# Strassen FFN weight sums moved from VectorE to accumulating DMA, with more FFN tiles in Strassen form

## The chip, the cores and the metric

One core of a Trainium2 chip runs the whole program. The metric is the device time of one execution in microseconds (us). TensorE (PE) multiplies, VectorE (DVE) and ScalarE (ACT) do elementwise work, GpSimd (POOL) does a little of it, and SyncE (SP) issues nearly all DMAs.

## The reference, cut to what matters

Two layers act on 512 latent tokens (x) and 256 context tokens (ctx), 1024 channels wide. Each has a mixer (four kinds of attention-like heads) and then a SwiGLU feed-forward network (FFN), which is what the change touches. In layer 1 only x goes through the FFN.

```python
def swiglu(h, w_ffn_in, w_ffn_out):          # 1024 -> 2 x 2816 -> 1024
    gate, up = jnp.split(h @ w_ffn_in, 2, axis=-1)
    return (jax.nn.silu(gate) * up) @ w_ffn_out

x = x + g2 * swiglu(modulate(rmsnorm(x, norm2), sh2, sc2), w_ffn_in, w_ffn_out)
if need_ctx:                                 # layer 0 only
    ctx = ctx + cg2 * swiglu(modulate(rmsnorm(ctx, norm2), csh2, csc2), w_ffn_in, w_ffn_out)
```

## The kernel before

Every float32 operand of a matrix product is scaled, split into a high and a low float16 part, and multiplied in three passes (high x high, high x low, low x high). Tokens stand in three groups of 256: group 0 is ctx, groups 1 and 2 are x.

**FFN weight tiles.** Each layer has 22 input tiles ("I", 128 hidden units: 1024 rows by 128 gate and 128 up columns) and 12 output tiles ("F", four column blocks by three chunks c of the hidden width). A tile is loaded by SP as two halves of 512 KB (`load_w`, `dma_thread2`); the F tiles of c = 2 have three row blocks instead of four, so their halves are 384 KB. At most four such halves of fast tiles are live at once (quota "wf", `wf1` = 4).

**Two ways to multiply a tile.** A *plain* tile is split by `split_thread` into float16 parts and multiplied by `p_ffn_in` (line 2168) or `p_ffn_out`: an input tile takes 48 matmuls of 128x256 for each group of tokens. A *fast* tile uses one level of Strassen-Winograd over its four quadrants A11, A12, A21, A22 and over token halves (x: group 1 against group 2; ctx: its own halves). `split_fast` builds seven operands: the quadrants A11, A12, A22 and the sums S1 = A21+A22, S2 = S1-A11, S3 = A11-A21, S4 = A12-S2. Each sum is one float32 `tensor_tensor` (`tto`, line 430; VectorE or GpSimd). Each operand is then split by `put`: a scaled cast to float16 (`cpo`, line 418 on ACT, or DVE) and one `scalar_tensor_tensor` for the low part (`sto`, line 434, DVE). `p_ffn_pair` (line 2208) and `p_out_pair` (line 2272) multiply: seven products of 12 matmuls, 84 in all, 256 columns wide for x and 128 for ctx, where a plain tile takes 96 for x. `pair_ev` (lines 2026 to 2039) and `resid_pair` (from line 995) join the products; `ffn_ev` (lines 2015 and 2016) ends a plain input tile. `pair_sums` and `hid_pair` make the sums on the token side.

**Which tiles are plain.** The tuple `cl` lists plain input tiles: three in layer 0, twelve in layer 1, so 15. Of the output tiles one is plain (layer 1, column block 3, c = 2).

**Order of the work.** `Plan.run` is a list scheduler that runs when the program is built. It holds a cost and a due time for each operation, picks an engine for operations that have several (`either`), and writes out a fixed order for each engine; each engine then runs its own order and waits at semaphores. Weight splits run ahead of the products: at most 16 tiles of split operands (quota "wh"; a fast tile takes four) exist at once. Where the scheduler foresees a gap of more than 0.4 us on PE, it fills it with dummy matmuls (`warm`, line 2466). So time on line 2466 is idle time of PE that looks busy.

Of the kernel before, what the change touches and what calls it, by code (L numbers as in the profile page):

```python
# [14 lines left out]
NL = 2  # L15
# [10 lines left out]
TUNE = {'pb': 2, 'pbr': 1, 's': 2, 'sr': 1, 't': 2, 'tr': 1, 'o': 3, 'orr': 1, 'bs': 6, 'bq': 4, 'p32': 3, 'sch': 4, 'lv': 3, 'pr_ap': 5, 'pr_av': 2, 'pr_cp': 7, 'pr_gate': 7, 'pr_bq': 10, 'pr_bv': 6, 'pr_du': 12, 'pr_ds': 6, 'pr_aatt': 6, 'pr_asc': 6, 'pr_catt': 10, 'pr_csc': 6, 'pr_gates': 2, 'pr_blev': 5, 'pr_bjoin': 4, 'pr_bst': 8, 'pr_bfin': 6, 'pr_norm': 0, 'pr_resid': 6, 'pr_split': 13, 'pr_prod': 20, 'win_prod': 16, 'pr_ffn': 1, 'pr_mod0': 3, 'pr_mod1': 1, 'win': 6, 'wmix': 8, 'wffn': 8, 'wkeep': 6, 'off1': 0, 'off2': 1, 'off0': 1, 'b_dve': 0.0, 'b_pool': 0.3, 'b_act': -0.2, 'm_pe': 0.0, 'm_el': 0.0, 'm1': 14, 'g2r': 2, 'pf': 8, 'wx': 2, 'wf1': 4, 'pr_ps': 2, 'x3': 2, 'jg': (1, 0), 'f32': ('B', 'B'), 'cl': ((0, 1, 19), (0, 1, 2, 3, 4, 6, 8, 10, 12, 14, 16, 18)), 'ofirst': 1, 'ostag': 0, 'clead': 0, 'ldma': 1.8, 'fgap': 0.4, 'fend': 0.1, 'hres': 3, 'bwh': 0.6, 'bws': 0.0, 'bpc': 0.0, 'bhh': 0.6, 'bhl': 0.0, 'pc': 3, 'flag': 1, 'pfr': 0, 'fst': 0, 'ord': 1, 'm0': 0, 'wsp': ((1, 1, 1, 1, 2, 1, 1, 1), (1, 1, 2, 1, 1, 1, 0, 2)), 'bwp': 0.3, 'bwl': 0.6, 'mcp': 1, 'm16': 0, 'm1n': 1, 'bmo': 1.5, 'bfu': 0.8, 'pr_rc': -1, 'ino': (2, 0), 'flag2': 4, 'mem': (28, 28), 'bfo': 0.0, 'pr_fin': 21, 'nlate': (1, 0, 1, 1, 1), 'bmc': 0.5}  # L26
# [25 lines left out]
W_OUT0 = 11  # L52

# [44 lines left out]
class Plan:  # L98
# [117 lines left out]
    def run(self):  # L216
        done, eng = self.done, self.eng
        while True:
# [56 lines left out]
            fin = end + (TUNE["ldma"] if e == "dma" else 0.0)  # L275
# [4 lines left out]
            for k in o.writes:  # L280
                done[k] = (fin, e)
# [55 lines left out]
def kernel(ctx: ExitStack, tc: tile.TileContext, xg, wall, wmod, pk32, pk16, dftx, dftc, out):  # L337
# [30 lines left out]
    modG = [const.tile([128, 2, 2, 8], F32, name=f"modG{l}") for l in range(NL)]  # L368
    lamt = const.tile([128, NL], F32, name="lamt")
# [76 lines left out]
    def load_w(l, i):  # L446
        n = w_rows(i)
        srcs = [wall[l, i, :, 0:n, :], wall[l, i, :, 4:4 + n, :]]
        add_load(("w", l, i), 2, None, None, srcs, ("wf", TUNE["wf1"] if fast(l, i) else 2))

    def dma_thread2():
        for key, n, shape, dt, srcs, quota, after in loads:
            ts = []
            if after:
                yield wait(*after)
            if key == "pk32b":
                yield op("dma", c_dma(4 * (NP32 - EARLY)), [], [key], lambda: nc.sync.dma_start(p32[:, EARLY:NP32], pk32[:, EARLY:NP32]))
                continue
            for i in range(n):
                if key[0] == "w":  # L460
                    t = yield alloc("g", [128, w_rows(key[2]), 256], F32, 0, quota)
# [28 lines left out]
    def split_fast(l, i):  # L490
# [3 lines left out]
        R = []  # L494
        A = {}
# [3 lines left out]
        def pair(a):  # L499
            for ab in PACK:  # L500
                if ab[0] == a:
                    t = yield alloc("g", [128, 2, 2, 4, 128], F16, w_reserve, ("wh", 16))
                    for u, name in enumerate(ab):
                        A[name] = t[:, u]
                        st["WT", l, i, name] = t
                    uses[id(t)] = users * len(ab)

        def put(name, src, key):
            yield from pair(name)
# [5 lines left out]
        st["A", l, i] = A  # L515
        yield wait(ld[0])
        R.append(st["ld", ("w", l, i), 0])
        a11, a21 = R[0][:, :, 0:128], R[0][:, :, 128:256]
        k = ("SS", l, i)
        yield from put("A11", a11, ld[0])  # L520
        yield wait(ld[1])
        R.append(st["ld", ("w", l, i), 1])
        a12, a22 = R[1][:, :, 0:128], R[1][:, :, 128:256]
        t = yield alloc("ff", [128, nr, 128], F32)
# [4 lines left out]
        t3 = yield alloc("ff", [128, nr, 128], F32)  # L529
        yield tto(n, [ld[0]], [k + (3,)], lambda: dict(out=t3, in0=a11, in1=a21, op=ALU.subtract), TUNE["bws"])  # L530
        yield from put("S3", t3, k + (3,))
        plan.free(t3)
        plan.free(R[0])
        yield from put("A12", a12, ld[1])
        yield tto(n, [("SA", l, i, "S2")], [k + (4,)], lambda: dict(out=t, in0=a12, in1=t, op=ALU.subtract), TUNE["bws"])
        yield from put("S4", t, k + (4,))
        plan.free(t)
        yield from put("A22", a22, ld[1])
        plan.free(R[1])

    WSP = {(l, i): TUNE["wsp"][l][min(i // 2, 7)] for l in range(NL) for i in range(NW)}

    def split_thread():
        for l in range(NL):
            for i in range(NW):
# [36 lines left out]
    def mod_chunk(l, c):  # L582
# [310 lines left out]
    def pair_sums(l, pr):  # L893
# [13 lines left out]
        for q in range(2):  # L907
# [5 lines left out]
            def make(n, o, x, y, rd):  # L913
                yield tto(2 * w, rd, [k + (n,)], lambda: dict(out=o, in0=x, in1=y, op=ALU.subtract))
# [4 lines left out]
            yield from make(1, a1, a2, a1, [hk[1, q], hk[2, q]])  # L919
            yield from make(3, a2, b2, a2, [hk[2, q + 2], k + (1,)])  # L920
            yield from make(2, a1, b2, a1, [("ST", l, pr, 1, q), hk[2, q + 2]])
# [51 lines left out]
    def add_to(x, p, j, l, g, src):  # L973
        kk = 2 * p + j
        return dict(out=x[:, j], in0=src, scalar=modG[l][:, 1, 1 if g == 0 else 0, kk:kk + 1], in1=x[:, j], op0=ALU.mult, op1=ALU.add)
# [12 lines left out]
    def resid_pair(l, p, c, pr):  # L988
# [10 lines left out]
        yield vop(c_dve(2 * w), [k + ("c",), k + ("P7",)], [k + ("u",)], lambda: V.tensor_tensor(out=t, in0=t, in1=Y, op=ALU.add))  # L999
# [14 lines left out]
        def f2():  # L1014
            V.scalar_tensor_tensor(**add_to(x2, p, 1, l, g2, v))
# [3 lines left out]
        def f3():  # L1019
            V.tensor_tensor(out=s[:, 0], in0=u, in1=Y[:, 1], op=ALU.add)  # L1020
            V.scalar_tensor_tensor(**add_to(x1, p, 1, l, g1, s[:, 0]))
# [930 lines left out]
    def hid_pair(l, j, pr):  # L1952
# [43 lines left out]
        yield tto(w, [k + (11,)] + ka, [k + ("t1",)], lambda: dict(out=a1, in0=a2, in1=a1, op=ALU.subtract))  # L1996
# [3 lines left out]
        yield from split(2 * w, (tc_[:, :, 0], tc_[:, :, 1]), a, [k + ("t2",)], k + (3,))  # L2000
# [19 lines left out]
    def pair_ev(l, m, X, Y, pr):  # L2020
# [5 lines left out]
        yield vop(c_dve(2 * w), [k + ("c",), k + ("P7",)], [k + ("u",)], lambda: V.tensor_tensor(out=c, in0=c, in1=Y, op=ALU.add))  # L2026
# [128 lines left out]
    def p_ffn_in(l, m, g):  # L2155
# [62 lines left out]
    def p_ffn_out(l, p, g, c):  # L2218
# [6 lines left out]
        for cb in range(2):  # L2225
            for j in js:
# [373 lines left out]
```

## Time and profile before

| | |
|---|---|
| median of 3 runs | 1724.01 us (1721.34 to 1727.58) |
| the profiled execution | 1723.17 us, span 1721.1 us |
| PE, DVE, ACT, POOL busy | 96%, 86%, 57%, 9% of the span |
| granted TensorE clock | 0.995 |
| moved by DMA | 201.43 MB |

An engine's busy time leaves out its waits. The FFN of layer 0 lies at about 490 to 1010 us of the span and that of layer 1 at about 1368 to 1700 us. The mixers lie before them.

### The profile page before, as it was taken

The page shows a single profiled execution, that of the slowest core. Times are in us where ns is not written, and L with a number is a line of the kernel's source. Part 1 is how long each engine was busy: PE and PEld are TensorE (multiplying, and loading weights), DVE is VectorE, ACT ScalarE, POOL GpSimd, SP SyncE. Part 2 cuts the span into 40 slices and gives each one's busy share as a digit, 9 for nine tenths or more (in the row PEclk, how much of TensorE's full clock was granted, in tenths as well). Part 3 has the DMA queues.
Part 4 walks back from the last instruction along what each step waited for, and adds up shares of the span by engine and source line. Part 5 has one row for each costly group of instructions (what it writes and reads, how often), then busy time and mean ns, then how long its engine had stood idle before and what let it go on. Part 6 is the DMA issues. An engine that isn't in the chain of part 4 may idle for free.

```text
span 1721.1 us, 45963 instructions
## 1 busy us (share of the span) xinstructions
PE 1660.1 (96%) x19718; PEld 1442.3 (84%) x19718; DVE 1484.4 (86%) x3141; ACT 979.6 (57%) x1766; POOL 149.7 (9%) x179
## 2 busy tenths in 40 slices
PE   8999998999999999999999999899889999999998
PEld 6678887887988788899889988788778888888887
DVE  6879899998589887899889998999997788888897
ACT  5637885566364553355435483678955555465454
POOL 0212111230000000000000013430010000000000
PEclk9999999999999999999999999999999999999999
DMA  9822111245135644522362351001113333462531
GB/s 368 334 83 79 59 46 52 86 149 185 50 124 187 193 148 122 174 75 63 111 193 72 112 179 36 14 27 50 51 51 123 136 95 102 127 193 75 184 124 50
DMA packets 62860, 201.43 MB, mean 117 GB/s; under 512 B 6848, under 2 KB 9152, under 8 KB 62656
## 3 DMA queue, kind: packets, MB, share of 16 engines
q1 hardware_dynamic: 62656, 198.50, 35.0%
q8 instruction: 154, 2.52, 0.6%
q14 instruction: 50, 0.41, 0.1%
HBM read 178.55 MB, written 19.92 MB: 115 GB/s over the span
## 4 chain that ended last, share of the span: by engine, by line
PE 59%; DVE 27%; ACT 6%; DMA 4%; issue 3%; POOL 1%; SPq 0%; DVEq 0%; ACTq 0%; POOLq 0%
PE ps L2208 15%; PE ps L2049 10%; DVE g L430 7%; PE ps L2168 7%; PE ps L2054 6%; PE ps L2272 5%; DVE g L434 4%; PE ps L616 2%; DMA g<-xsc 2%; PE ps L2466 2%; PE ps L1218 2%; DVE pl L430 1%; ACT g L418 1%; PE ps L1158 1%; DVE g L1548 1%
## 5 line engine op out<-in xcount | busy, mean ns | idle before, releaser
L430 DVE TENSOR_TENSOR g<-g,g 128x512 f32<-128x512 f32 (+7 forms) x698 | 439.9, 656 | 46.8 <-ACT g L416 34.4
L418 ACT ACTIVATE g<-g 128x512 f16<-128x512 f32 (+2 forms) x391 | 241.5, 642 | 236.3 <-DVE g L430 230.6
L2208 PE MATMUL ps<-g,g 128*128 128x256 f16 (+1 forms) x4032 | 361.4, 251 | 0.0
L2208 PEld LDWEIGHTS <-g 128*128 128x128 f16 x4032 | 326.2, 98 | 38.3 <-issue 10.9
L434 DVE SCALAR_TENSOR_TENSOR g<-g,g 128x512 f16<-128x512 f32 (+4 forms) x442 | 300.4, 696 | 59.0 <-ACT g L418 56.0
L2049 PE MATMUL ps<-g,g 128*128 128x256 f16 x2256 | 271.8, 273 | 1.8 <-DVE g L434 1.5
L2272 PEld LDWEIGHTS <-g 128*128 128x128 f16 x2709 | 226.0, 98 | 32.9 <-issue 8.2
L2049 PEld LDWEIGHTS <-g 128*128 128x128 f16 x2256 | 217.9, 98 | 29.2 <-DVE g L434 2.1
L2272 PE MATMUL ps<-g,g 128*128 128x256 f16 (+1 forms) x1917 | 211.0, 269 | 8.3 <-DVE g L999 3.6
L416 ACT CAST g<-g 128x512 f16<-128x512 f32 (+3 forms) x269 | 162.5, 615 | 76.3 <-DVE g L430 46.4
L2054 PE MATMUL ps<-g,g 128*128 128x256 f16 x1632 | 198.2, 274 | 0.0
L2054 PEld LDWEIGHTS <-g 128*128 128x128 f16 x1632 | 157.2, 98 | 31.3 <-issue 10.7
L2168 PE MATMUL ps<-g,g 128*128 128x256 f16 x1584 | 175.7, 273 | 0.0
L2168 PEld LDWEIGHTS <-g 128*128 128x128 f16 x1584 | 154.8, 98 | 18.9 <-issue 0.8
L416 ACT COPY g<-ps 128x512 f32<-128x512 f32 (+4 forms) x163 | 94.0, 583 | 120.2 <-PE ps L2272 23.7
L1198 ACT ACTIVATE g<-ps 128x512 f32<-128x512 f32 x156 | 91.6, 596 | 31.8 <-PE ps L1232 23.1
L430 DVE TENSOR_TENSOR pl<-g,ph 128x512 f16<-128x512 f32 x137 | 93.0, 694 | 7.1 <-ACT ph L416 6.7
L430 DVE TENSOR_TENSOR g<-g 128x256 f32<-128x256 f32 (+3 forms) x197 | 88.9, 460 | 2.4 <-ACT g L754 1.8
L430 POOL TENSOR_TENSOR g<-g,g 128x256 f16<-128x256 f32 (+4 forms) x17 | 23.5, 1385 | 695.0 <-ACT g L416 579.1
L416 ACT CAST ph<-g 128x512 f16<-128x512 f32 (+2 forms) x141 | 80.3, 572 | 4.7 <-DVE g L430 1.0
L2466 PE MATMUL ps<-p16c 128*128 128x256 f16 x595 | 75.5, 279 | 3.8 <-DMA p16c<-in_pk_dram 3.8
L2466 PEld LDWEIGHTS <-p16c 128*128 128x128 f16 x595 | 58.9, 101 | 15.8 <-issue 4.2
(248 smaller groups left out, 2220.2 us busy)
## 6 DMA issues: line engine op xcount, KB each, us to landing
g<-in_wall_dram SPq DMA_DIRECT2D x180, 512.0 KB, 4.4
g<-in_wmod_dram SPq DMA_DIRECT2D x96, 512.0 KB, 6.7
g<-xsc SPq DMA_DIRECT2D x40, 256.0 KB, 5.2
xsc<-g SPq DMA_DIRECT2D x40, 256.0 KB, 3.0
g<-in_xg_dram SPq DMA_DIRECT2D x12, 512.0 KB, 6.7
g<-in_wall_dram SPq DMA_DIRECT2D x16, 384.0 KB, 3.4
xsc<-g SPq DMA_DIRECT2D x10, 512.0 KB, 2.8
g<-xsc SPq DMA_DIRECT2D x10, 512.0 KB, 5.1
```

The source lines that it names most:

```text
L416: S.copy(o, i)
L418: S.activation(out=o, in_=i, func=AF.Copy, scale=scale)
L430: return either(r, w, ("dve", c_dve(n), lambda: V.tensor_tensor(**f()), bias, True), ("pool", c_pool(n), lambda: G.tensor_tensor(**f()), 0 ...
L434: return vop(c_dve(n), r, w, lambda: V.scalar_tensor_tensor(**f()), True)
L616: T.matmul(bank[32 * cg:32 * cg + 32, :], lhsT=cst[:, 2 * (4 * kr + cg):2 * (4 * kr + cg) + 32], rhs=ts[cg // 2][:, cg % 2, :], start=(kr ...
L1198: yield aop(c_act(512), [k], [k + (0,)], lambda pp=pp, bank=bank: S.activation(out=pp, in_=bank, func=AF.Exp, scale=scale), "exp")
L2049: T.matmul(bank[:, cb, :], lhsT=W[a][:, kw, 128 * cb:128 * cb + 128], rhs=xh[b][:, kx, :], start=(first and n == 0), stop=(last and n == 2 ...
L2054: T.matmul(bank[:, t, :], lhsT=xh[b][:, k, 128 * t:128 * t + 128], rhs=wt[a][:, k, :], start=(first and n == 0), stop=(last and n == 2), s ...
L2168: T.matmul(bank[:, cb, :], lhsT=wt[a][:, k % 4, :], rhs=xh[b][:, k % 4, :], start=(k == 0 and n == 0), stop=(k == 7 and n == 2), skip_grou ...
L2208: T.matmul(into[name], lhsT=wt[:, y, kk, :], rhs=x[:, z, kk, :], start=(name in ("P1", "P6") and kk == 0 and n == 0), stop=(kk == 3 and n ...
L2272: T.matmul(o, lhsT=wt[:, y, j % 4, :], rhs=x[:, z], start=(name in ("P1", "P6") and j == js[0] and n == 0), stop=(j == js[-1] and n == 2), ...
L2466: T.matmul(t[:, 0:256], lhsT=ident16, rhs=p16[:, 128:384], start=True, stop=True)
```

## The change

The two halves of a fast tile are laid out by quadrant in DRAM (a new input `wffn`), so that a quadrant is one contiguous run of each partition. Three of the four sums no longer have tiles of their own: GpSimd issues DMAs that read a quadrant from DRAM again and add it to what lies in SBUF. On the upper half R[0], A11 is split first, then A21 is added to it in place (S3); in the other place of R[0], which holds A21, A22 is added (S1), then A11 (S2), then A12 (S4), each after the operand before it has been split. An accumulating DMA only adds, so the signs of some operands turn; the token sums and the joining operations turn with them (`subtract` for `add`, a negated gate vector `modN`, scalar `-IWS`). In `hid_pair` one subtraction over two blocks becomes two operations of half the width. The scheduler books such a DMA as 1.5 us of GpSimd's time (`acp`) and 3.0 us until it has landed (`acl`). The list `cl` of plain input tiles becomes two in layer 0 and four in layer 1, so 6 instead of 15.

```diff
-'jg': (1, 0), 'f32': ('B', 'B'), 'cl': ((0, 1, 19), (0, 1, 2, 3, 4, 6, 8, 10, 12, 14, 16, 18))
+'acp': 1.5, 'acl': 3.0, 'whq': 16, 'pr_sp': 12, 'jg': (1, 0), 'f32': ('B', 'B'), 'cl': ((0, 1), (0, 1, 2, 3))
...
+        def quad(h, q):
+            return wffn[l, i - W_FFN0, :, h, q, 0:nr, :]
...
+        def acc(dst, src, rd, key):
+            yield ("op", (("pool", TUNE["acp"], lambda: G.dma_start(dst, src, accum_op=ALU.add), 0.0, False, None, TUNE["acl"]),), rd, [key])
...
+        def first():
+            a = R[0][:, 0]
+            k = ("SS", l, i, 3)
+            yield from put("A11", a, ld[0])
+            yield from acc(a, quad(0, 1), [("SA", l, i, "A11")], k)
+            yield from put("S3", a, k)
+            over(0)
+
+        def chain():
+            t = R[0][:, 1]
+            k = ("SS", l, i)
+            yield from acc(t, quad(1, 1), [ld[0]], k + (1,))
+            yield from put("S1", t, k + (1,))
+            yield from acc(t, quad(0, 0), [("SA", l, i, "S1")], k + (2,))
+            yield from put("S2", t, k + (2,))
+            yield from acc(t, quad(1, 0), [("SA", l, i, "S2")], k + (4,))
+            yield from put("S4", t, k + (4,))
+            over(0)
...
-        yield tto(n, ld, [k + (1,)], lambda: dict(out=t, in0=a21, in1=a22, op=ALU.add), TUNE["bws"])
-        yield from put("S1", t, k + (1,))
-        yield tto(n, [("SA", l, i, "S1")], [k + (2,)], lambda: dict(out=t, in0=t, in1=a11, op=ALU.subtract), TUNE["bws"])
-        yield from put("S2", t, k + (2,))
...
-        yield tto(n, [ld[0]], [k + (3,)], lambda: dict(out=t3, in0=a11, in1=a21, op=ALU.subtract), TUNE["bws"])
-        yield from put("S3", t3, k + (3,))
...
-        yield tto(n, [("SA", l, i, "S2")], [k + (4,)], lambda: dict(out=t, in0=a12, in1=t, op=ALU.subtract), TUNE["bws"])
-        yield from put("S4", t, k + (4,))
...
-        yield tto(2 * w, [k + (1,)] + kb + ([k + (12,)] if tail else []), [k + ("t2",)], lambda: dict(out=a, in0=b2.unsqueeze(1).to_broadcast([128, 2, w]), in1=a, op=ALU.subtract))
+        yield tto(w, [k + ("t1",)] + kb + ([k + (12,)] if tail else []), [k + ("t3",)], lambda: dict(out=a2, in0=a2, in1=b2, op=ALU.subtract))
+        yield tto(w, [k + (1,)] + kb, [k + ("t2",)], lambda: dict(out=a1, in0=a1, in1=b2, op=ALU.add))
```

## Rows read from the trace of the kernel before

**Rows 1.** Page, busy time, share of span and instructions of each engine
```profile
span 1721.1 us, 45963 instructions
PE 1660.1 (96%) x19718; PEld 1442.3 (84%) x19718; DVE 1484.4 (86%) x3141; ACT 979.6 (57%) x1766; POOL 149.7 (9%) x179
```

**Rows 2.** Busy time of each engine in both FFN stretches (layer 0, layer 1)
```profile
core 0: us, PE busy (x) PEld busy (x) DVE busy (x) ACT busy (x) POOL busy (x), PEclk, DMA share, GB/s
490.00:1010.00 520.00, 512.41 (x5888) 454.98 (x5887) 457.88 (x1023) 258.13 (x555) 3.55 (x4) 1.00 0.43 135
1368.00:1690.00 322.00, 318.97 (x2908) 284.06 (x2907) 279.49 (x520) 165.54 (x308) 0.70 (x1) 1.00 0.39 123
```

**Rows 3.** The same stretches, the dummy matmuls of line 2466 alone
```profile
490.00:1010.00 520.00, 21.84 (x179) 17.30 (x179) 1.00 0.43 135
1368.00:1690.00 322.00, 15.49 (x127) 12.42 (x127) 1.00 0.39 123
```

**Rows 4.** Groups of matmuls by line and form: count, busy us, mean ns
```profile
L2208 PE MATMUL ps<-g,g 128*128 128x256 f16 x2436 | 274.9, 273 | 0.0
L2168 PE MATMUL ps<-g,g 128*128 128x256 f16 x1584 | 175.7, 273 | 0.0
L2208 PE MATMUL ps<-g,g 128*128 128x128 f16 x1596 | 92.9, 219 | 0.0
```

**Rows 5.** Groups on DVE by line and form
```profile
L430 DVE TENSOR_TENSOR g<-g,g 128x512 f32<-128x512 f32 x321 | 216.7, 684 | 13.8 <-ACT g L754 3.8 <-ACT g L416 3.7 <-ACT g L1582 2.7
L434 DVE SCALAR_TENSOR_TENSOR g<-g,g 128x512 f16<-128x512 f32 x315 | 211.8, 686 | 51.8 <-ACT g L418 50.9
L430 DVE TENSOR_TENSOR g<-g,g 128x1024 f16<-128x1024 f32 x53 | 64.5, 1219 | 8.5 <-ACT g L416 7.9
L430 DVE TENSOR_TENSOR g<-g 128x256 f32<-128x256 f32 x99 | 41.1, 418 | 2.3 <-ACT g L754 1.8
L434 DVE SCALAR_TENSOR_TENSOR g<-g,g 128x512 f32<-128x512 f32 x29 | 19.9, 688 | 1.7
L2026 DVE TENSOR_TENSOR g<-g,ps 128x512 f32<-128x512 f32 x29 | 19.7, 680 | 3.0 <-PE ps L2208 3.0
L2016 DVE SCALAR_TENSOR_TENSOR g<-ps,g 128x256 f32<-128x256 f32 x33 | 13.8, 417 | 1.9 <-ACT g L2015 1.7
L2036 DVE TENSOR_TENSOR g<-g,ps 128x256 f32<-128x256 f32 x29 | 12.0, 415 | 2.0 <-PE ps L2208 2.0
L430 DVE TENSOR_TENSOR g<-g,g 128x384 f32<-128x384 f32 x21 | 11.5, 550 | 0.1
L430 DVE TENSOR_TENSOR g<-g 128x128 f32<-128x128 f32 x42 | 11.3, 283 | 0.1
L423 DVE CAST g<-g 128x512 f16<-128x512 f32 x36 | 15.0, 423 | 2.7 <-ACT g L416 1.5 <-ACT g L864 0.7
```

**Rows 6.** Groups on ACT by line and form
```profile
L418 ACT ACTIVATE g<-g 128x512 f16<-128x512 f32 x314 | 188.3, 625 | 209.9 <-DVE g L430 204.2 <-DVE g L434 4.1 <-issue 1.1
L561 ACT ACTIVATE g<-g 128x1024 f32<-128x1024 f32 x60 | 63.0, 1051 | 6.6 <-DMA g<-in_wall_dram 6.6
L416 ACT CAST g<-g 128x1024 f16<-128x1024 f32 x50 | 52.2, 1044 | 1.0
L416 ACT COPY g<-ps 128x512 f32<-128x512 f32 x101 | 57.9, 582 | 46.7 <-PE ps L616 13.5 <-PE ps L1808 13.3 <-PE ps L2272 6.6
```

**Rows 7.** Waits of ACT, layer 0 stretch, then layer 1: us, times, longest
```profile
ACT g L418 <- DVE g L430: 125.1, 86, 4.7
...
ACT g L418 <- DVE g L430: 104.1, 72, 3.9
```

**Rows 8.** The DMA queue of SP, then issues: count, KB, median us to landing
```profile
q1 hardware_dynamic: 62656, 198.50, 35.0%
...
g<-in_wall_dram SPq DMA_DIRECT2D x180, 512.0 KB, 4.4
g<-in_wmod_dram SPq DMA_DIRECT2D x96, 512.0 KB, 6.7
g<-xsc SPq DMA_DIRECT2D x40, 256.0 KB, 5.2
...
g<-in_dftc_dram SPq DMA_DIRECT2D x1, 256.0 KB, 2.4
```

**Rows 9.** Waits of DVE for residual loads, and of PE: us, times, longest
```profile
DVE g L1010 <- DMA g<-xsc: 7.1, 7, 1.7
...
PE ps L2272 <- DVE g L999: 3.6, 2, 1.8
...
PE ps L2272 <- DVE g L430: 2.5, 2, 1.5
```

**Rows 10.** Timeline of PE at the end of layer 0: start us, us
```profile
1001.66 8.13 PE L2466 MATMUL ps<-p16c 128*128 128x256 f16 x73
```

More of the change, by code (lines that the diff above doesn't have):

```diff
@@ L274, in run @@
             end = start + cost
-            fin = end + (TUNE["ldma"] if e == "dma" else 0.0)
+            fin = end + (best[2][6] if len(best[2]) > 6 else TUNE["ldma"] if e == "dma" else 0.0)
             eng[e] = end
@@ L280, in run @@
             for k in o.writes:
-                done[k] = (fin, e)
+                done[k] = (fin, "dma" if len(best[2]) > 6 else e)
             th = o.th
@@ L336, with kernel @@
 @with_exitstack
-def kernel(ctx: ExitStack, tc: tile.TileContext, xg, wall, wmod, pk32, pk16, dftx, dftc, out):
+def kernel(ctx: ExitStack, tc: tile.TileContext, xg, wall, wffn, wmod, pk32, pk16, dftx, dftc, out):
     nc = tc.nc
@@ L368 @@
     modG = [const.tile([128, 2, 2, 8], F32, name=f"modG{l}") for l in range(NL)]
+    modN = [const.tile([128, 2, 8], F32, name=f"modN{l}") for l in range(NL)]
     lamt = const.tile([128, NL], F32, name="lamt")
@@ L447, in load_w @@
         n = w_rows(i)
-        srcs = [wall[l, i, :, 0:n, :], wall[l, i, :, 4:4 + n, :]]
+        srcs = [wffn[l, i - W_FFN0, :, h, :, 0:n, :] if i >= W_FFN0 else wall[l, i, :, 4 * h:4 * h + 4, :] for h in range(2)]
         add_load(("w", l, i), 2, None, None, srcs, ("wf", TUNE["wf1"] if fast(l, i) else 2))
@@ L460, in dma_thread2 @@
                 if key[0] == "w":
[L461 removed]
+                    t = yield alloc("g", [128, 4, 256] if key[2] < W_FFN0 else [128, 2, w_rows(key[2]), 128], F32, 0, quota)
                 else:
@@ L498, in split_fast @@
         users = 2 if l == 0 else 1
[L499 to L506, printed above, removed]
+        A = st["A", l, i] = {}
+        R = [None, None]
+        left = [2, 2]
+        def quad(h, q):
+            return wffn[l, i - W_FFN0, :, h, q, 0:nr, :]
         def put(name, src, key):
-            yield from pair(name)
+            yield wait(("pk", l, i, name))
             dst = A[name][:, :, 0:nr]
@@ new lines, in over @@
+        def over(h):
+            left[h] -= 1
+            if not left[h]:
+                plan.free(R[h])
+        def first():
[15 more added lines that the diff above has]
+            over(0)
@@ new lines, in other @@
+        def other():
+            yield from put("A12", R[1][:, 0], ld[1])
+            over(1)
+            yield from put("A22", R[1][:, 1], ld[1])
+            over(1)
+        yield wait(ld[0])
+        R[0] = st["ld", ("w", l, i), 0]
+        plan.spawn(first(), TUNE["pr_sp"])
+        plan.spawn(chain(), TUNE["pr_sp"])
+        for u, ab in enumerate(PACK):
+            if u == 2:
+                yield wait(ld[1])
+                R[1] = st["ld", ("w", l, i), 1]
+                plan.spawn(other(), TUNE["pr_sp"])
+            t = yield alloc("g", [128, 2, 2, 4, 128], F16, w_reserve, ("wh", TUNE["whq"]))
+            for v, name in enumerate(ab):
+                A[name] = t[:, v]
+                st["WT", l, i, name] = t
+                plan.done["pk", l, i, name] = (0.0, "none")
+            uses[id(t)] = users * len(ab)
@@ L971, in x_back, with add_to @@
             plan.free(x)
-    def add_to(x, p, j, l, g, src):
+    def add_to(x, p, j, l, g, src, neg=False):
         kk = 2 * p + j
-        return dict(out=x[:, j], in0=src, scalar=modG[l][:, 1, 1 if g == 0 else 0, kk:kk + 1], in1=x[:, j], op0=ALU.mult, op1=ALU.add)
+        return dict(out=x[:, j], in0=src, scalar=(modN[l] if neg else modG[l][:, 1])[:, 1 if g == 0 else 0, kk:kk + 1], in1=x[:, j], op0=ALU.mult, op1=ALU.add)
     def resid_ffn(l, g, p, c, bank, bkey):
@@ L2552 @@
     fo = f["w_ffn_out"].reshape(L, NM, 128, 4, 256).transpose(0, 3, 2, 1, 4)
-    for i in range(11, NW):
+    fi = fi.reshape(L, NM, 128, 2, 4, 2, 128).transpose(0, 1, 2, 3, 5, 4, 6)
+    for i in range(W_FFN0, NW):
         kind, p, c = w_tile(i)
         if kind == "I":
-            wall[:, i] = fi[:, p]
-        elif kind == "F":
+            wffn[:, i - W_FFN0] = fi[:, p]
+        else:
             for h in range(2):
                 b = fo[:, p, :, 8 * c + h:min(8 * c + 8, NM):2]
-                wall[:, i, :, 4 * h:4 * h + b.shape[2]] = b
+                n = b.shape[2]
+                wffn[:, i - W_FFN0, :, h, :, 0:n] = b.reshape(L, 128, n, 2, 128).transpose(0, 1, 3, 2, 4)
     wm = f["w_mod"]
```

65 lines of the change are left out of this document (26 added, 39 removed).

## The prediction

> **What bounds the kernel now.** I read the page's engine totals first: PE is busy 96% of the span, DVE 86%, ACT 57% [rows 1]. The change lies in the two FFN stretches, so I cut the trace there. In layer 0, 512.4 of 520 us are PE work, in layer 1 319.0 of 322 [rows 2]; but dummy matmuls stand for 21.8 and 15.5 us of that [rows 3]. So PE does real work in 490.6 of 520 and 303.5 of 322 us: it is the bound in both, and 29.4 + 18.5 = 47.9 us is all that other engines cost it there. DVE is next, at 457.9/520 = 88% and 279.5/322 = 87%; ACT half idle, GpSimd all but empty [rows 2]. The reader should see two separate stakes: PE work, which is paid in full, and PE's 47.9 us of loss, of which only some can come from DVE.
>
> **PE, the tiles that turn fast.** Nine input tiles change (19 in layer 0; 4, 6, 8, 10, 12, 14, 16, 18 in layer 1). Plain matmuls removed: 3 x 48 + 8 x 96 = 912. One costs 175.7/1584 = 110.9 ns of PE [rows 4] (busy over count, since a single one overlaps its neighbours), so -101.2 us. Added: 9 x 84 = 756 of 256 columns at 274.9/2436 = 112.9 ns, +85.3, and 84 of 128 columns for ctx at 92.9/1596 = 58.2 ns, +4.9 [rows 4]. Sum **-11.0 us**, -9.4 of it in layer 1. PE is the bound in both stretches, so this goes to the end unless something new is late.
>
> **DVE, the sums.** Before, 31 fast tiles in layer 0 and 21 in layer 1 have four sums each: 180 of 512 elements at 0.684 us, 28 of 384 at 0.550 [rows 5]: -123.1 - 15.4 = -138.5 us, 82.7 in layer 0 and 55.8 in layer 1. (GpSimd is nearly empty in both stretches, so these are DVE's.)
>
> **DVE, what comes back.** A tile that turns fast adds for x seven low parts (7 x 0.686) and a longer joining (0.680 + 0.418 + two of 0.415 + 0.688), in all 7.42 us, and drops two low parts of 1024 (2 x 1.219) and two ends (2 x 0.417), 3.27 us [rows 5]: +4.15 each, +37.3 for nine. The ctx part of tile 19 adds about 1.3. The subtraction that becomes two in `hid_pair` costs 2 x 0.418 - 0.684 = 0.15 for each of 22 x pairs and 2 x 0.283 - 0.418 = 0.15 for 11 ctx pairs [rows 5]: +5.0. Net -138.5 + 43.6 = **-95 us of DVE**: about -74 in layer 0 (88% to 76%) and -21 in layer 1 (87% to 84% of a shorter stretch). ACT per new tile: 7 x 0.625 + 0.582 - 2 x 1.051 - 2 x 1.044 = +0.77 [rows 6], 7 us in all, off the path at half idle. The sign turns swap operations of equal kind; the negated gate adds four tiny operations: nothing. The token-side pairs already exist in both layers.
>
> **What DVE's relief is worth.** Of PE's 47.9 us of loss some 10 lie at the end of layer 0, where the norm of the next layer is waited for (a run of 73 dummies begins at 1001.7 us [rows 10]); the sums are long done there. Of the other 37 the trace gives no single owner, since the scheduler filled foreseen gaps. Bounds: nothing and 37. ACT's casts wait 125.1 + 104.1 = 229 us for sums [rows 7], so DVE is a real brake on the preparation, but that runs tiles ahead of PE. I take a third, **-12 us**, nearest to layer 0's share, where most DVE time is freed.
>
> **The accumulating DMAs.** After, 61 fast tiles give 244 of them, 216 of 256 KB and 28 of 192 KB: 62 MB read again on top of 201. No row shows one. *Landing:* the scheduler books 1.5 + 3.0 = 4.5 us. The nearest rows are a 256 KB load at a quiet time, 2.4 us, and 256 KB loads of the residual stream among other traffic, 5.2 us median [rows 8]. I take 4.5. At 5.2 the casts wait 244 x 0.7 = 171 us, less than the 229 us that go with the old sums [rows 7]; at 2.4 they gain slack. What queues behind a late one on ACT is the PSUM copies and silu on which PE's next products depend; on GpSimd only the next accumulations, since it does next to nothing else in these stretches [rows 2].
>
> *Engine time:* the main queue's 198.50 MB took 35.0% of 1721 us, so 3.03 us a MB and 0.795 us for 256 KB [rows 8]. Call an accumulation's price k times that. k = 1 if it runs like a load; k = 3 if the source read, the read of what lies there and the write all cost a pass. Layer 1 uses 0.39 x 322 = 126 us now [rows 2] and gains 104 x 0.795 + 12 x 0.596 = 90k; layer 0 uses 224 and gains 99k. I take k = 1.5, between the bare load and a doubled read: 261 of about 307 us, 85%, in layer 1, and 373 of about 503 in layer 0. No bound, but loads land later. DVE waits for residual loads already, 7.1 us on the first reader alone [rows 9]; I charge **+4 us** for more of that (bounds 0 and 7, the row doubled).
>
> The Trainium skill (DMA: Bandwidth & Descriptors, Anatomy of one DMA — SWDGE (gpsimd) path) gives 2.0 us plus bytes over 436 GB/s for a DMA that GpSimd issues; my estimate from that page is 2.6 us for 256 KB. By it every accumulation lands inside the 4.5 us, and the +4 would fall away: 1700 instead of 1704. No run here shows it yet.
>
> A cast of 512 elements takes DVE 423 ns against 684 for a two-input add of the same length [rows 5]: casts run faster, and DVE may be given more of them now that it has room. The Trainium skill (SBUF — State Buffer, Who interferes with whom) says that a DVE copy or cast in a two-port mode locks GpSimd out of the port with which it writes DMA descriptors. This speaks against the change; if each of the 244 waited out one such cast, by the rows that would be 244 x 0.42 = 103 us spread over GpSimd, which has 840 idle, and still a landing of 4.9 us: late waits of 98 us against the 229 removed. So by this rule the sum stays; it is one more step toward the second rival below.
>
> **Sum.** -11.0 - 12 + 4 = -19 us. The profiled execution took 1723.2 us (span 1721.1), 0.8 under the median of the runs, so 1723 - 19 = **1704 us**, -1.1%. A measurement of this kernel tells a change from none at about 0.3%, 5 us.
>
> **Rivals.**
> 1. *The DMA engines become the bound in layer 1.* 126 + 90k exceeds the stretch's old 322 us plus layer 0's gain (about 9) from k = 2.3. At k = 2.5 layer 1 takes 351 us, +29, less 9 in layer 0: **1743 us**; at k = 3 it is 396, +74: about 1790. For it: the bytes are read, added and written in place. Against: each quadrant is one run of 2 KB a partition, and 61% of the engines' time in layer 1 is free now [rows 2]. Chance 0.15.
> 2. *Late landings stall ACT in order.* At 5.7 us the casts wait 244 x 1.2 = 293 us, 64 more than the sums cost now; a quarter of that reaching PE gives +16: **1720 us**, no change. Chance 0.12. Beyond 6.2 us (244 x 1.7 = 415, all of ACT's 418 idle us in the two stretches [rows 2]) it turns slower, e.g. at 6.4 us (244 x 1.9 - 418 = +46) 1750. The 512 KB loads that come in fours land at 6.7 us [rows 8], so this isn't far off. Chance 0.07.
> 3. *DVE owned most of the loss.* All 37 us come back, no new waits: 1723 - 11 - 37 = **1675 us**; half-way, 1690. For it: ACT's 229 us of waits for DVE. Against: PE's own longest waits for DVE in the output products are 3.6 and 2.5 us in all [rows 9]. Chance 0.08.
>
> **How the numbers follow.** Forecast 0.58 (1692 to 1716: the recovery from 20 to 3 us, the charge from 0 to 7). Faster is forecast plus rival 3, 0.66; same 0.12; slower 0.15 + 0.07 = 0.22. With a tenth or so left out at either end the range is 1690 (rival 3's middle) to 1745 (rival 1 at k = 2.5).
>
> **What would show it.** Right: line 2168 at 672 matmuls and line 2208 at 3192 + 1680; the 512-element adds of line 430 down by about 135 + 45; DVE about 1390 us busy; dummy matmuls and gaps in the FFN stretches about a quarter smaller; the accumulations landing in 4 to 5 us; the DMA share in layer 1 at 0.75 to 0.9. Wrong: a DMA share near 1 there (rival 1); the row "ACT line 418 waits for DMA" above 300 us together with PE waiting for ACT (rival 2); an FFN of layer 0 shorter by over 20 us (rival 3). My softest step is the landing time, since no row shows this kind of DMA.

## The result, and the profile after

The changed kernel takes 1831.2 us (median of 4 runs, 1822.5 to 1833.5), against 1725.8 for the kernel before beside it: ratio 1.0605, 95% interval 1.0563 to 1.0647. The forecast was 1704 us and the range ended at 1745. All four sums of a fast tile go by accumulating DMA (4 x 61 = 244), not three of the four. The first lines of the page after, which answer to [rows 1], with its DMA queues:

```profile
span 1829.8 us, 46220 instructions
PE 1670.9 (91%) x19458; PEld 1433.1 (78%) x19458; DVE 1404.7 (77%) x3058; ACT 974.7 (53%) x1794; POOL 361.9 (20%) x426
...
q1 hardware_dynamic: 64704, 198.50, 32.2%
q0 software_dynamic: 35136, 62.14, 21.0%
```

DVE did lose 80 us of work, and yet the span grew by 108.7 us: PE, DVE and ACT are each busy for a smaller share of it than before, and GpSimd, which now issues these DMAs, for 20%. So none of them became the bound; they wait for one another. The two FFN stretches, and the dummy matmuls alone in them, which answer to [rows 2, 3] (columns as there):

```profile
490.00:1057.00 567.00, 515.05 (x5723) 449.03 (x5721) 387.51 (x924) 240.06 (x533) 114.47 (x135) 0.95 0.72 177
1428.00:1808.00 380.00, 325.09 (x2788) 280.43 (x2785) 270.60 (x530) 179.24 (x360) 99.32 (x116) 0.93 0.80 182
```

```profile
490.00:1057.00 567.00, 0.93 (x7) 0.64 (x7) 0.95 0.72 177
1428.00:1808.00 380.00, 3.24 (x20) 2.22 (x20) 0.93 0.80 182
```

There are hardly any dummies left (0.9 us against 21.8 in layer 0, 3.2 against 15.5 in layer 1): the scheduler foresaw a PE without gaps. The trace has 52 and 55 us of gaps there. The order was written for a run that didn't happen. Who waited is in the view of waits (us in all, times, longest); the landings are in the view of the accumulations' line:

```profile
ACT g L420 <- DMA g<-in_wffn_dram: 350.2, 164, 11.2
...
DVE g L436 <- ACT g L420: 180.6, 108, 7.8
...
PE ps L2234 <- ACT g L418: 31.6, 6, 9.7
...
PE ps L2298 <- DVE g L1024: 25.6, 8, 6.8
```

```profile
DMA to landing us min/median/max: 3.5/6.6/13.2
```

Line 420 is the scaled cast of an operand (418 before), 436 the low part behind it, 418 now the casts without a scale and the PSUM copies (416 before), 2234 and 2298 the FFN products. The casts waited 350 us for quadrants, where they had waited 229 us for sums [rows 7]. An accumulation was booked to land 4.5 us after its issue; the median is 6.6, the longest 13.2. How one late landing reaches PE is seen in the timeline of layer 1 (start us, us, then the engine; the bracket is the idle time before it and who ended it):

```profile
1517.83 1.15 ACT L420 ACTIVATE g<-g 128x512 f16<-128x512 f32 x2 [0.30 <-DMA g<-in_wffn_dram]
...
1523.34 0.63 ACT L420 ACTIVATE g<-g 128x512 f16<-128x512 f32 x1 [3.27 <-DMA g<-in_wffn_dram]
1523.87 0.57 ACT L418 COPY g<-ps 128x512 f32<-128x512 f32 x1
1524.00 0.69 DVE L436 SCALAR_TENSOR_TENSOR g<-g,g 128x512 f16<-128x512 f32 x1 [1.97 <-ACT g L420]
1524.49 3.78 PE L2234 MATMUL ps<-g,g 128*128 128x256 f16 x17 [7.42 <-ACT g L418]
```

ACT stands 3.27 us before a cast that PE doesn't need yet: its low part on DVE ends at 1524.69, when PE is running again. Right behind it in ACT's order is a PSUM copy that PE does need; PE stands for 7.42 us. And the clock falls in such a gap (columns as in [rows 2]; of the last three numbers the first is the granted clock, the second the share of the DMA engines):

```profile
1510.00:1520.00 10.00, 5.09 (x44) 4.10 (x43) 9.28 (x20) 5.98 (x13) 3.43 (x4) 0.95 0.80 148
1520.00:1530.00 10.00, 5.51 (x30) 3.93 (x29) 7.44 (x15) 4.79 (x10) 3.43 (x4) 0.53 0.92 166
1530.00:1540.00 10.00, 9.11 (x82) 7.79 (x80) 9.49 (x20) 7.43 (x16) 3.43 (x4) 1.00 0.84 160
```

In and behind that idle time the granted clock is 0.53 over 10 us, so mostly the lower of its two levels (1.2 GHz instead of 2.4); it is full again once PE has been busy.

### The profile page after: what moved, and what is told of

Same layout as the page of the kernel before. It is cut to its first block, busy times and chain, and to the rows that moved or that the text cites. A ratio compares the mean times of both kernels' runs of the same rounds, so it can differ in the third digit from the quotient of the medians.

```text
span 1829.8 us, 46220 instructions
## 1 busy us (share of the span) xinstructions
PE 1670.9 (91%) x19458; PEld 1433.1 (78%) x19458; DVE 1404.7 (77%) x3058; ACT 974.7 (53%) x1794; POOL 361.9 (20%) x426
## 3 DMA queue, kind: packets, MB, share of 16 engines
q0 software_dynamic: 35136, 62.14, 21.0%
## 5 line engine op out<-in xcount | busy, mean ns | idle before, releaser
L2234 PE MATMUL ps<-g,g 128*128 128x256 f16 (+1 forms) x4872 | 468.3, 260 | 51.4 <-ACT g L418 31.6
L436 DVE SCALAR_TENSOR_TENSOR g<-g,g 128x512 f16<-128x512 f32 (+4 forms) x514 | 346.3, 696 | 189.1 <-ACT g L420 180.6
L420 ACT ACTIVATE g<-g 128x512 f16<-128x512 f32 (+2 forms) x449 | 272.9, 638 | 361.5 <-DMA g<-in_wffn_dram 350.2
L432 DVE TENSOR_TENSOR g<-g,g 128x512 f32<-128x512 f32 (+6 forms) x555 | 321.3, 611 | 59.2 <-ACT g L418 47.5
L514 POOL DMA_DIRECT2D g<-in_wffn_dram x244 | 210.4, 967 | 706.2 <-DVE g L436 447.3
L2075 PE MATMUL ps<-g,g 128*128 128x256 f16 x2256 | 273.2, 273 | 1.8 <-DVE g L436 1.5
L2298 PE MATMUL ps<-g,g 128*128 128x256 f16 (+1 forms) x1917 | 225.2, 280 | 48.7 <-DVE g L1024 25.6
L2080 PE MATMUL ps<-g,g 128*128 128x256 f16 x1632 | 197.3, 273 | 0.2 <-DVE g L432 0.2
L418 ACT CAST g<-g 128x512 f16<-128x512 f32 (+3 forms) x243 | 140.7, 590 | 62.2 <-DVE g L432 31.6
L2194 PE MATMUL ps<-g,g 128*128 128x256 f16 x672 | 74.7, 273 | 0.0
L1607 ACT ACTIVATE g<-g 128x512 f32<-128x512 f32 x80 | 47.1, 637 | 41.6 <-DVE g L1575 41.5
L1243 PEld LDWEIGHTS <-ph 128*128 128x128 f16 x1248 | 63.4, 97 | 6.5 <-DVE pl L432 1.7
## 6 DMA issues: line engine op xcount, KB each, us to landing
g<-in_wffn_dram SPq DMA_DIRECT2D x16, 384.0 KB, 6.4
```

The costliest lines, as they stand in the source:

```text
L418: S.copy(o, i)
L420: S.activation(out=o, in_=i, func=AF.Copy, scale=scale)
L432: return either(r, w, ("dve", c_dve(n), lambda: V.tensor_tensor(**f()), bias, True), ("pool", c_pool(n), lambda: G.tensor_tensor(**f()), 0 ...
L436: return vop(c_dve(n), r, w, lambda: V.scalar_tensor_tensor(**f()), True)
L514: yield ("op", (("pool", TUNE["acp"], lambda: G.dma_start(dst, src, accum_op=ALU.add), 0.0, False, None, TUNE["acl"]),), rd, [key])
L1243: T.matmul(bank[:, u, t, :], lhsT=a[:, i, q], rhs=v[:, b, :], start=(n == 0), stop=(n == 6 * nk - 1))
```

## The experiments

Theory A, formed on this trace: late landings against the booking, in orders that can't change, are the loss. Theory B, a rival: an accumulation costs the DMA engines too much, and they are full in layer 1 (their share is 0.80 over the stretch, 0.91 from 1500 to 1700 us). Theory C, another: the extra fast tiles, or three accumulations in a row, are too much for the load buffers. All medians follow with the length of each layer's FFN, read on PE's timeline of the profiled execution from the first plain input matmul to the end of the last output product of a fast tile (in layer 1 the one plain output tile, 8 us, follows). "Booked" is the scheduler's number until a landing (`acl`), on top of the 1.5 us that it books for GpSimd.

| kernel | what it is | median us | FFN 0 | FFN 1 |
|---|---|---|---|---|
| before | | 1724 to 1726 | 510.0 | 331.3 |
| after | the change | 1831.2 | 567.2 | 379.9 |
| e1 | 6.0 us booked | 1740.2 | 519.4 | 338.0 |
| e2 | DMA alone, 15 plain | 1823.3 | 568.0 | 373.8 |
| e3 | tiles alone, DVE sums | 1780.6 | 510.6 | 384.0 |
| e4 | copies, not accumulations | 1723.2 | 505.7 | 330.9 |
| e5 | 9.0 us booked | 1782.3 | 543.9 | 354.8 |
| e6 | 6.0 booked, 15 plain | 1752.4 | 527.9 | 342.2 |
| e7 | two of four sums by DMA, 6.0 | 1718.3 | 507.8 | 324.4 |
| e8 | 6.0 booked, six buffers | 1764.4 | 544.3 | 327.9 |
| e9 | no sums, 15 plain | 1711.3 | 502.8 | 321.6 |
| e10 | no sums, 6 plain | 1687.3 | 497.7 | 307.3 |
| e11 | e7 with 3.0 booked | 1754.2 | 524.1 | 347.3 |
| e12 | e7 with 15 plain | 1733.2 | 521.1 | 334.9 |
| e13 | e10 + traffic, buffers held | 1792.3 | 533.5 | 366.5 |
| e14 | e7 with 4.5 booked | 1724.6 | 509.3 | 331.7 |
| e15 | e10 + traffic into scratch | 1750.5 | 534.6 | 327.3 |
| e16 | e10, smaller pool (control of e15) | 1693.8 | 493.7 | 305.7 |
| e17 | e7, SP's DMAs booked 4.0, not 1.8 | 1703.5 | 497.1 | 317.0 |
| e18 | before, SP's DMAs booked 4.0, not 1.8 | 1718.8 | 501.0 | 334.1 |

### Booking: e1_acl6 and e4_copy

```diff
-'acl': 3.0
+'acl': 6.0
```

> The changed kernel with one number changed: the scheduler books 6.0 us instead of 3.0 until an accumulating DMA has landed (7.5 with the 1.5 us of GpSimd; the trace of the changed kernel has a median landing of 6.6 to 6.7 us, longest 13.2). Theory A (booking): the loss comes from ACT's and DVE's fixed order, written for landings at 4.5 us, so that casts wait in front of work that PE needs. Then an order written for 7.5 us takes most of the 106 us back: 1715 to 1750 us, waits of line 420 for the quadrants from 350 to below 150 us. Theory B (throughput): an accumulation costs the DMA engines twice a load (21.0% of the span for 62 MB against 32.2% for 198.5 MB, so 6.2 against 3.0 us a MB), and the engines are full in layer 1 (share 0.89 to 0.93): no order helps, over 1800 us.

```diff
-G.dma_start(dst, src, accum_op=ALU.add)
+G.dma_start(dst, src)
```

> The changed kernel with plain copies in the place of the accumulations: the same DMAs from GpSimd, the same bytes from DRAM, order, waits and bookings, but the quadrant replaces what lies there instead of being added (left out: the additions, so S1 to S4 are single quadrants). It measures what accumulating costs beyond a GpSimd DMA. Theory B: the queue of GpSimd falls from 21% to about 11% of the span, landings to 4.5 to 5 us, time 1705 to 1740. Theory A: landings of GpSimd DMAs stay above the booked 4.5 us because of the issue and of shared queues, by about half of the lateness: 1750 to 1790. If accumulating itself costs nothing, 1831 as the changed kernel.

e1 changes no DMA and only the written order: 1740.2 us (ratio 1.0097, interval 1.0076 to 1.0118). So 91 of some 106 us come back by the order alone, and theory A holds for most of the loss. e4 keeps the order of the change, instruction for instruction, and makes the DMAs faster (the copies replace what lies there, so the sums are left out): 1723.2 us, like before (0.9998, 0.9984 to 1.0012). All of the loss comes back, but e4 alone doesn't tell A from B, since the landing and the DMA engines' time change together. Waits and landings in e1, each from its own view, then the landings of the copies in e4, and its page's lines of the engines and of GpSimd's queue:

```profile
ACT g L420 <- DMA g<-in_wffn_dram: 173.2, 114, 9.4
```

```profile
DMA to landing us min/median/max: 3.5/6.6/12.1
```

```profile
DMA to landing us min/median/max: 2.7/4.6/10.5
```

```profile
PE 1639.0 (95%) x19458; PEld 1419.0 (82%) x19458; DVE 1401.6 (81%) x3058; ACT 971.8 (56%) x1794; POOL 282.4 (16%) x426
...
q0 software_dynamic: 19072, 62.14, 11.0%
```

In e1 the landings are just as late (6.6 us); the casts wait half as much because they stand later. Only 113.6 us of these 173 are for accumulations, where it was 348.5 in the change; the rest is for SP's weight loads, which land late too (6.6 us in the median). In e4 the landings meet the 4.5 us that were booked. Since after and e4 run the same order, their PE lines split the loss: PE is busy 31.9 us longer in after for the same matmuls (1670.9 against 1639.0), most of it the price of the lower clock in and behind gaps (the mean granted clock is 0.967 against 0.988), and not busy for 158.9 instead of 82.1 us, 76.8 more.

### The two halves of the change: e2_acc15 and e3_dve6

```diff
-'cl': ((0, 1), (0, 1, 2, 3))
+'cl': ((0, 1, 19), (0, 1, 2, 3, 4, 6, 8, 10, 12, 14, 16, 18))     # e2, in the changed kernel
-'cl': ((0, 1, 19), (0, 1, 2, 3, 4, 6, 8, 10, 12, 14, 16, 18))
+'cl': ((0, 1), (0, 1, 2, 3))                                      # e3, in the kernel before
```

> The changed kernel with the 15 plain input tiles of before: the accumulating DMA alone. Accumulations fall from 244 to 208, in layer 1 from 116 to 80, in layer 0 from 128 to 124 with a like number after. Theory A (booking): each late landing costs about the same everywhere, so the loss falls with their number, by 36 of 244: 1731 + 0.85 x 95 = about 1810 us. Theory B (throughput, worst in layer 1): layer 1's engine load falls to 126 + 134 = 260 of 322 us, below full; its share of the loss goes and 40 to 50 us of layer 0 stay: 1765 to 1785 us. If the nine added fast tiles were the whole cause, about 1715.

> The kernel before with 6 plain input tiles instead of 15: the second part of the change alone, the sums stay on VectorE. PE work falls by 11 us. DVE gains nine times 4.15 us and 36 more sums of 0.68 us, 63 us in all, 57 of them in layer 1, where it is at 279 of 322 us: 336 of 312, so DVE becomes the bound there. If so: 1735 to 1760 us. If GpSimd and ACT take enough over: 1712 to 1725.

The DMA alone costs nearly everything: 1823.3. Theory B as the main cause falls here: layer 1 has a third fewer accumulations, its DMA share is 0.67, and 42 us of loss remain there; layer 0, where the share is only 0.72 in the change, loses 58. The tiles alone cost 57 us, more than expected, all of it in layer 1: DVE, at 87% there [rows 2], can't make the sums of eight more tiles in time (336 us of DVE work there in e3, and 629 dummy matmuls where before has 127). So the two halves need each other; neither is good alone.

### How much to book: e5_acl9, e6_acl6_15, e8_wf6

```diff
-'acl': 3.0
+'acl': 9.0                                   # e5
+'acl': 6.0, and 'cl' with 15 plain tiles     # e6
+'acl': 6.0, and 'wf1': 6                     # e8
```

> The changed kernel with 9.0 us booked until an accumulation has landed (10.5 with GpSimd's 1.5; longest landing seen 13.2 in the changed kernel, 12.1 with 6.0 booked). Theory A (booking): the waits of line 420 for quadrants, 350 us at 3.0 and 173 at 6.0, fall below 80; what is left of the loss at 6.0 (1740 against 1723.6) was lateness too, so 1715 to 1730. Theory C (chains): each tile's three accumulations in a row then take over 30 us in the written order, the four load buffers hold the upper halves that long and weights come too late by plan: 1750 or more, with more dummy matmuls.

> 6.0 us booked and the 15 plain input tiles of before: accumulations for the sums at an honest booking, without the nine new fast tiles. PE does 11 us more than with 6 plain tiles, but 36 accumulations fewer share the DMA engines, nearly all in layer 1. If layer 1's full DMA engines (share 0.9 and more with 6.0 booked) cause what is left of the loss there (338 against 331 us): 1730 to 1740, layer 1's FFN below 335 us. If what is left is PE work and chains: 1745 to 1755.

> 6.0 us booked and six load buffers of fast tiles live at once instead of four (two tiles to three). Theory C (chains): the upper half is held through three accumulations in a row, so with four buffers the loads come late; two more give back most of what is left at 6.0: 1715 to 1730. If the DMA engines' load or lateness is what is left: 1735 to 1745, unchanged.

At 9.0 the casts wait only 116 us, but the kernel is slower than at 6.0: dummy matmuls rise from 453 to 979.

```profile
L2492 PE MATMUL ps<-p16c 128*128 128x256 f16 x979 | 119.1, 277 | 3.8 <-DMA p16c<-in_pk_dram 3.8
```

So the scheduler itself now foresees weights that come late: three accumulations in a row at 10.5 us are too long a chain, as theory C has it. Of the 116 us only 47.7 are for accumulations. e6 isn't faster but slower than e1, by 12 us, and layer 1 (342.2 against 338.0) too: the nine tiles help, and relieving the DMA engines there doesn't. Six buffers instead of four (e8) help layer 1 (327.9) and hurt layer 0 by 25 us, with 766 dummies instead of 453; why the order there came out worse wasn't traced. Theory C's simple remedy doesn't help.

### Fewer accumulations: e7_two, e11_two_acl3, e14_two_acl45, e12_two15

```diff
-            yield from acc(t, quad(0, 0), [("SA", l, i, "S1")], k + (2,))
+            yield tto(n, [("SA", l, i, "S1")], [k + (2,)], lambda: dict(out=t, in0=t, in1=R[0][:, 0], op=ALU.add), TUNE["bws"])
...
-            yield from acc(t, quad(1, 0), [("SA", l, i, "S2")], k + (4,))
+            yield tto(n, [("SA", l, i, "S2"), ld[1]], [k + (4,)], lambda: dict(out=t, in0=t, in1=st["ld", ("w", l, i), 1][:, 0], op=ALU.add), TUNE["bws"])
```

> 6.0 us booked, 6 plain tiles, and only S1 and S3 by accumulating DMA, both straight from the load; S2 and S4 are added in place by tensor_tensor again (122 of them, about 80 us of DVE, of the 138 that the change took away plus its nine tiles). 122 accumulations instead of 244 and one in a row instead of three. If the number of accumulations in a row and the engines' load are what is left at 6.0: 1705 to 1722, faster than before, since PE does 11 us less. If DVE is then the bound in layer 1 (about 258 + 40 of 322 us): 1725 to 1745.

> e7_two (S1 and S3 by accumulating DMA, S2 and S4 on DVE, 6 plain tiles) with 3.0 us booked instead of 6.0. Theory A (booking): the wrong booking hurts with one accumulation in a row too: 122 landings at about 6 us against 4.5 booked, about half of the changed kernel's waits, so 1745 to 1775. Theory C (chains): only accumulations in a row add up their lateness, so with one link 1718 to 1728.

> e7_two with 4.5 us booked, so that 1.5 + 4.5 meets the median landing of 6.1 us that e7_two shows. With 3.0 it took 1754.2, with 6.0 1718.3. Theory A (booking): half of the landings are later than the order expects, so some of the loss comes back: 1722 to 1740. If a booking at the median is as good: 1712 to 1720.

> e7_two with 15 plain tiles: 104 accumulations, two sums of each tile on DVE. Against e7_two (1718.3) it measures the nine new fast tiles at a working state. If PE's 11 us go to the end: 1727 to 1732, slower than before's 1724, so that the gain of e7_two is the tiles. If the gain is DVE's relief: 1710 to 1718.

With two accumulations a tile, never two in a row, the change beats the kernel before: 1718.3 us (0.9964, 0.9952 to 0.9976). At the old booking of 3.0 the same kernel takes 1754.2, at 4.5 (6.0 with GpSimd's 1.5; the median landing is 5.8) 1724.6. So a booking at the median isn't enough; nearly half of the landings are later. e7 has both fewer accumulations and fewer in a row; which of the two makes the difference to e1 wasn't separated. With 15 plain tiles it takes 1733.2: the gain is the nine tiles, as the sum of the prediction had it.

### The floor: e9_free15 and e10_free6

```diff
...
-            yield from acc(t, quad(1, 1), [ld[0]], k + (1,))
-            yield from put("S1", t, k + (1,))
-            yield from acc(t, quad(0, 0), [("SA", l, i, "S1")], k + (2,))
-            yield from put("S2", t, k + (2,))
+            yield from put("S1", t, ld[0])
+            yield from put("S2", t, ld[0])
...
```

> The sums left out altogether (each operand S1 to S4 is split straight from a loaded quadrant: no add on VectorE, no accumulating DMA, no wait for either), with the 15 plain tiles of before. It measures what taking the sums off DVE is worth when nothing takes their place; the prediction put -12 us on this, between nothing and -37. If DVE owned most of PE's loss in the FFN: 1690 to 1700. If PE was the bound and the gaps have other owners: 1716 to 1724.

> The sums left out altogether as in e9_free15, with 6 plain tiles. Against e9_free15 it measures the nine new fast tiles where nothing waits for sums: by the sum of the prediction 11 us less (9.4 of it in layer 1's FFN). It is the floor for every way of making the sums: 1695 to 1712. If the longer joining of the fast tiles on DVE and ACT eats the 11 us: the same as e9_free15.

Both leave the sums out and split the loaded quadrants as they are. Taking the sums off DVE with nothing in their place is worth 14.3 us (1711.3 beside 1725.6; the new layout and the rest of the change are in it); the prediction said 12. The nine tiles are worth 23.9 more, where it said 11: the FFN matmul lines fall by 14.7 us of PE, and the rest wasn't traced. So 38 us were to be had, and the change stands 144 us above this floor.

### What the traffic itself costs: e13_traffic6, e15_scratch, e16_free6_g26

e13 adds the 244 accumulations to the floor kernel behind the readers; e15 adds them on scratch places; e16 is e15 without them.

```diff
             yield from put("S4", t, ld[0])
+            yield from acc(t, quad(1, 1), [("SA", l, i, "S1"), ("SA", l, i, "S2"), ("SA", l, i, "S4")], k + (1,))    # e13, and two more behind it
...
+            dst = scrt[j % 4][:, 0:nr]                                                                             # e15
+            ... G.dma_start(dst, src, accum_op=ALU.add) ...
```

> The floor kernel (operands split straight from the loaded quadrants, 6 plain tiles, 1687.3 us) plus all 244 accumulating DMAs, 6.0 us booked, issued on the same places after their readers are done: the same traffic, the same three in a row, the load buffers held as long, but no cast waits for a sum (left out: the sums in the operands). If readers that wait in a fixed order are the price (theory A): 1687 to 1700. If the DMA engines' load and the held buffers are: 1715 to 1740, as e1_acl6 (1740.2).

> The floor kernel (sums left out, operands split from the loaded quadrants, 6 plain tiles) plus all 244 accumulating DMAs at about the times of the changed kernel, but into four scratch places that nobody reads and no load uses (pool g2 26 instead of 28 to make room). Only GpSimd waits for them. If late landings cost time only through what waits for them: 1687 to 1702, as the floor. If the engines' load as such slows the weight loads and with them PE (share of 21% more of the span): 1720 and more.

> The floor kernel with pool g2 at 26 instead of 28 tiles and no DMA added: the control for e15_scratch. 1685 to 1692 if the pool has room to spare.

e13 broke theory A in its narrow form, in which only the readers of a sum pay. No cast reads a sum there, and it takes 1792.3 us. Its waits (SP's queue, then ACT, then, from the view of the accumulations, who waited for them):

```profile
SPq L468 <- DMA g<-in_wffn_dram: 160.3, 20, 16.4
...
ACT g L420 <- DMA g<-in_wffn_dram: 152.1, 40, 11.2
```

```profile
  ACT g L420: 99.2, 23
```

SP's next weight load stands until the accumulations in its buffer have landed, 20 times and up to 16.4 us, and casts then wait for the load. More than half of the casts' waits, though, are for the accumulations themselves. Loads and split operands take their places from one pool (`alloc("g", ...)`), so a cast may stand until the accumulations in the place that it writes have landed; that this is the dependency isn't shown. So e13 doesn't set the traffic apart from late landings. A late landing costs through anything that is queued behind it in a fixed order, a load as well as a cast. In e15 nothing reads or reuses the places, and 56.7 us are lost all the same against its control (1750.5 and 1693.8), so B is part of the truth; e1, too, stands 53 us above the floor. The trace shows where:

```profile
DVE g L1045 <- DMA g<-xsc: 52.1, 14, 9.3
...
PE ps L2308 <- DVE g L1034: 40.5, 7, 12.3
...
DVE g L1050 <- DMA g<-xsc: 23.3, 11, 6.6
```

```profile
g<-xsc SPq DMA_DIRECT2D x40, 256.0 KB, 7.6
```

The loads of the residual stream (xsc) land at 7.6 us in the median instead of 5.1 in the control, DVE waits 75 us for them, and PE waits behind DVE. Those loads were booked at 2.5 us (0.7 for the transfer and 1.8). The accumulations of e15 run in denser bursts than those of the change (a DMA share of 0.9 and more in ten slices of its page after the start, seven in that of the change), so 57 us is no exact share of its loss.

### Booking the other loads: e17_two_ld4 and e18_before_ld4

```diff
-'ldma': 1.8
+'ldma': 4.0
```

> e7_two (1718.3 us) with 4.0 us instead of 1.8 booked until one of SP's DMAs has landed. If residual loads that land later than booked are what the traffic costs there: 1700 to 1712, DVE's waits for them (14 us on the first reader) halved. If they are not, or if loads booked later delay the order by as much: 1715 to 1730.

> The kernel before with 4.0 us instead of 1.8 booked for SP's DMAs, the control for e17. Its waits for residual loads are small (7 us on the first reader), so 1720 to 1728, no change.

Booking 4.0 instead of 1.8 us for SP's DMAs takes e7 from 1718.3 to **1703.5 us** (0.9884 of before, 0.9863 to 0.9905): the fastest kernel here that makes its sums. That this is also the figure forecast for the change is chance: it is another kernel. The control gains 0.3% (1718.8; 0.9970, 0.9960 to 0.9980). So the same booking is worth 15 us with the accumulations and 6 without them. DVE's waits for residual loads (its first reader) halve from 14.0 to 7.0 us; what else the later booking of all of SP's DMAs changed in the order wasn't traced.

## Why the prediction was wrong, step by step

- **PE's work, -11.0: right in kind.** The counts came out as written (672 matmuls on the plain line, 3192 + 1680 on the fast one). Measured at three working points the nine tiles are worth 12.2 (e6 to e1), 14.9 (e12 to e7) and 23.9 us (e9 to e10); at the change's own booking of 3.0 they cost 7.9 (e2 to after).
- **DVE, -95: 80 measured.** The sums went. With them gone the scheduler gave DVE some more casts, 11 more of 512 and 1024 elements, some 5 us; the rest of the difference wasn't traced.
- **DVE's relief, -12: 14.3 measured in e9.** The third that was taken was a fair guess.
- **Landing, 4.5 us taken: 6.6 to 6.7 measured. This is the first step that failed.** It was bounded by 2.4 and 5.2 us from plain loads [rows 8], and the value was put where the scheduler's own number was; that number is no measurement. Both bounds were of the wrong kind: an accumulation lands 2.0 us later than a copy by the same engine (6.6 against 4.6 in e4), so it lay beyond the upper one. The Trainium skill's fit (DMA: Bandwidth & Descriptors, Anatomy of one DMA — SWDGE (gpsimd) path), 2.6 us for 256 KB by my estimate, agrees with the quickest copy (2.7) and with no accumulation: the quickest took 3.5. The measurement decides.
- **"+4 for late loads": mis-sized.** e15 puts the traffic's price at 57 us in its own arrangement, and booking SP's loads later takes 15 us off e7. Loads of the residual stream were already booked too early before, as [rows 9] hinted.
- **The waits that replace the old ones, put at nothing: the second step that failed.** I set 244 x lateness against the 229 us of waits for sums and ACT's idle time, as if idle time anywhere could hold a wait. In after ACT waits only 350 us for quadrants and is idle for 47% of the span, and still PE stands behind it. Idle time in a fixed order covers only a wait that falls into it; the timeline shows a wait just ahead of a copy that PE needs. Two runs show this step apart from the landing. In e4 the copies land at 4.6 us, nearly as taken, and it takes 1723.2 us and not 1704: of the 127 us between forecast and measurement 108 come with accumulating (its landing and engine time together), and 19 stay. In e2 the accumulations land at 5.7 us, where the second rival gave 1720, and it takes 1823.3.
- **The clock wasn't in the sum.** Unforeseen gaps have no dummies, the clock falls, and the same matmuls take longer; that is most of the 31.9 us between after and e4.
- **The rivals.** The second one was the true mechanism, with its point (6.2 us) below the landing that came; its slower half had a chance of 0.07. Its sign came: ACT waited 350 us for the DMA (above the 300), and PE 31.6 for ACT. By its formula 6.7 us gives 1704 + 244 x 2.2 - 418 = 1823 us. That this is near the measured time is luck: its terms aren't (537 us of waits against 350), and 6.6 us gives 1798. The first had its premise right, k = 2.08 (6.18 against 2.97 us a MB; 1.5 was taken), but e2 and e6 show that a full queue in layer 1 wasn't what decided, and its sign, a share near 1 there, didn't come (0.80, as forecast). The port rule that the prediction took from the Trainium skill (SBUF — State Buffer, Who interferes with whom) left no mark: an accumulation holds GpSimd 0.86 us in the median, and 210 us in all. Few issues fell on a copy or cast of DVE, so the rule was hardly put to the test.

Left open: the clock's share outside of after and e4, and how the price divides between late readers, late buffers and late residual loads in the change itself; the runs show that the order, the buffers and the other loads matter, not how their prices add. The change with all its accumulations and both bookings (6.0 for them, 4.0 for SP's DMAs) was not run, so whether four of them a tile can win isn't known.

## What to carry to other kernels

When a statically ordered kernel moves work to a DMA, measure that DMA's landing in the traffic that it will make, and book it at the slow half of the landings rather than at the median (e7 against e14), but not so late that chains of them hold up the plan (e5). A wait that lands late costs what is queued behind it in order, not the idle time of its engine. Few such links, none behind another, paid here (e7), and so did booking every other load anew (e17), since the new traffic delays those too. Two changes that only pay together (here: fewer sums on DVE, more fast tiles) should also be judged against the floor in which the cost is left out: it tells what is at stake before the cost is argued.

## What the runs showed of the hardware

An accumulating DMA from DRAM into SBUF occupied the DMA engines 2.03 times as long as a copy of the same bytes by the same engine (21.0% of 1829.8 us against 11.0% of 1721.1), in 35136 against 19072 packets, 144 against 78 for each DMA. The price of a MB, 6.2 us, is the same with half as many of them (e7: 31.07 MB, 11.3% of 1711.2 us), so it doesn't come from their number. An accumulation held GpSimd 0.86 us against 0.54 at its issue and landed, in this traffic, 2.0 us later in the median, 0.8 us at the quickest.
